# Attention scores in a one-core Fourier and latent-attention layer: three full-array passes replaced by two full ones and one on 32 rows, with queries and keys made earlier and parked in DRAM

## The chip, the cores and the metric

The kernel runs on one core of a Trainium2 chip. The metric is the device time of one execution in microseconds (us). The kernel before takes 936.31 us, the median of three runs (936.22 to 936.6).

## What is computed

One layer of a diffusion backbone on 1024 latent and 128 context tokens. Two branches leave one input projection: a Fourier mix over positions and channels, gated and mapped to 1024 channels (the output map), and latent attention with 8 heads. Both are merged with sigmoid gates, projected once more, added to the input and normalised. The part that the change touches is this:

```python
def mla_attention(q_nope, q_rope, k_nope, k_rope, v):
    ...
        s = jnp.einsum('bqhd,bkhd->bhqk', qn, k_nope) + jnp.einsum('bqhr,bkr->bhqk', qr, k_rope)
        p = jax.nn.softmax(s.astype(jnp.float32) * scale, axis=-1).astype(v.dtype)
        return jnp.einsum('bhqk,bkhd->bqhd', p, v)
...
def merge_out(x, gate, u_f, z_f, attn, z_a, g_f, g_a, w_f_out_l, w_a_out_l, w_out_l):
    y_f = (fourier_mix(u_f) * jax.nn.silu(z_f)) @ w_f_out_l
    y_a = (attn * jax.nn.silu(z_a)) @ w_a_out_l
    merged = jax.nn.sigmoid(g_f) * y_f + jax.nn.sigmoid(g_a) * y_a
    return x + gate * (merged @ w_out_l)
```

A head has 64 channels without position (nope) and 32 rotary channels (rope) in queries and keys. Latent queries see 128 cached context keys and 1024 latent keys; the 128 context queries see 128 context keys.

## The kernel before

Every matrix product is made to nearly float32 accuracy out of rounded halves: an operand x is split into hi (x rounded) and lo (x minus hi), and `mm3` (line 121) issues three TensorE passes, hi by hi, hi by lo and lo by hi, into one PSUM bank (lines 122, 125 and 126). A pass loads 128 columns of weights (LDWEIGHTS, PEld in the profile) and streams up to 512 columns past them. A Python program writes the instructions down; a list scheduler then sets each engine's order. It may bring later instructions ahead of one that waits, for a free PSUM bank say. There are eight PSUM banks (`MM`, line 101), and 43 SBUF buffers of 4.6 KB per partition (`U`, line 86) that tiles take in turn.

The stages in order of time: the input side, Fourier transform and gate projections (up to about 421 us); the **Fourier output map** (`for m in range(8)`, from line 1027); **attention** (8 heads); the **merge** (`merge_part`, line 1288); the last projection. SyncE (SP) issues nearly all DMAs, in one order.

The output map has 8 blocks m of 3 column thirds c, each 12 passes of 384 columns. Between the thirds stand other pieces: `low_tr` (line 947) transposes the latent rows of one token tile and makes the operands cqh, cql, kvh, kvl and the rotary key rows; `k_up` makes the nope keys of two heads (head pair 0 here), `q_chunk` the queries of a head for 384 tokens (head 0, first third, here), `value_map` the values. The residual gate's rows are made here too, by `ada_rows` (line 228): 8 products at four positions of 32 array columns, and `gate_row`.

Attention runs by head. A head has 9 steps of 128 queries; eight of them score three thirds of 384 keys (`Step.score`, line 1091), the ninth scores the context. Each third takes the three passes of `mm3`, with all 128 rows in use: 64 nope rows, 32 rotary rows times cosine and 32 swapped rotary rows times sine; the weights are the queries and the keys stream. VectorE (DVE) takes the minimum (line 1099), ScalarE (ACT) the exponential (line 1110), TensorE transposes the result (line 1131), ACT and DVE split it (lines 1132 and 109), TensorE multiplies with the values (lines 1151 and 1152). The strings `HSEQ` and `LSEQ` set the order in which a head's pieces are written. During a head h, `q_chunk` (Q in the string) makes the queries still missing and those of head h+1, `k_up` and `k_split` (K) the next keys, with splits on GpSimd (POOL).

Of the kernel before, what the change touches and what calls it, by code (L numbers as in the profile page):

```python
# [17 lines left out]
P = 128  # L18
# [41 lines left out]
VS = (3, 0, 0)  # L60


@with_exitstack
def kernel(ctx: ExitStack, tc: tile.TileContext, a: dict):
# [376 lines left out]
    def split_w(src, shape):  # L441
        raw = U(shape, F32, "wr")
        nc.sync.dma_start(raw, src)
        return split(raw)
# [7 lines left out]
    low_d = dram.tile([9, P, 448], F32, name="low_d")  # L452
# [54 lines left out]
    def low_out(c, pss):  # L507
# [8 lines left out]
        for j, ps in enumerate(pss):  # L516
            t = 3 * c + j
            row = H([P, 448], s="low")
            xk = ps[:, 384:416].rearrange("p (a b i) -> p a b i", a=2, b=2)
            if t < 8:  # L520
# [6 lines left out]
                for r in range(2):  # L527
                    dve.tensor_tensor(out=row[:, 384 + 32 * r : 416 + 32 * r], in0=t2.rearrange("p a b i -> p (a b i)"),
                                      in1=t1.rearrange("p a b i -> p (a b i)"), op=ALU.add)
            else:  # L530
                for r in range(2):
# [318 lines left out]
    def low_load(i):  # L850

        rows = U([P, 2, 448], s="low")
        for e in range(2):
# [3 lines left out]
            else:  # L857
                nc.sync.dma_start(row[:, 256:384], a["cache_ckv"])
                nc.sync.dma_start(row[:, 384:416], a["cache_krope"])
                nc.sync.dma_start(row[:, 416:448], a["cache_krope"])  # L860
# [26 lines left out]

    for i, (kind, dst, blk, m) in enumerate(PAIRS):
# [12 lines left out]

    gate_d = dram.tile([2, D], F32, name="gate_d")
    grow = [U([2, D], F32, "grow") for _ in range(2)]
    nc.sync.dma_start(grow[1], a["b_gate"].to_broadcast([2, D]))

    def load_gate(j):
        parts = []
        for q in range(4):
            w = U([P, 2, 512], s="wgate")
            nc.sync.dma_start(w, a["w_gate"][j, q])  # L910
            parts.append(w)
        return parts

    def gate_row(rows, j):
        ps = MM()
        pe.matmul(ps[0:2, :], sel, rows, start=True, stop=True)
        sl = slice(j * 512, (j + 1) * 512)
        dve.tensor_tensor(out=grow[0][:, sl], in0=ps[0:2, :], in1=grow[1][:, sl], op=ALU.add)
        if j == 1:
            nc.sync.dma_start(gate_d, grow[0])  # L920

# [4 lines left out]
    KB = [(U([P, NT], F32R, "kh"), U([P, NT], F32R, "kl")) for _ in range(2)]  # L926
    KC = [(C([P, P], F32R, "kch"), C([P, P], F32R, "kcl")) for _ in range(2)]
# [5 lines left out]
    def put_kv(ckvn, krd, kv_h, kv_l, kb, sl, gain=True):  # L933
# [3 lines left out]
        pe.transpose(pt[0:64, 128:256], krd, ident)  # L937
# [5 lines left out]
        for h, l in kb:  # L943
            act.copy(h[64:128, sl], pt[0:64, 128:256])
            dve.tensor_tensor(out=l[64:128, sl], in0=pt[0:64, 128:256], in1=h[64:128, sl].bitcast(F32), op=ALU.subtract)

    def low_tr(t, row):
        sl = slice(t * P, (t + 1) * P)
        ckn, kd = row[:, 256:384], row[:, 384:448]
        if t == 9:  # L950
            put_kv(ckn, kd, kvh[:, 1024:1152], kvl[:, 1024:1152], KB, slice(1024, 1152), False)
            return
        if t < 8:
            put_kv(ckn, kd, kvh[:, sl], kvl[:, sl], KB, sl)
        else:
            put_kv(ckn, kd, kch, kcl, KC, slice(0, 128))
# [14 lines left out]
    def k_up(wk, c, kf):  # L971
# [5 lines left out]
        mm3(ps[:, 0:n], wk[:, 0, :], wk[:, 1, :], rh, rl, True, True)  # L977
        for e in range(2):
            x = H([64, CH], s="kf") if e == 0 else None
            x = x[:, 0:n] if e == 0 else (kf[0][:, sl] if c < 3 else kf[1])  # L980
            act.copy(x, ps[64 * e : 64 * e + 64, 0:n])  # L981
            if e == 0:
                k_split(0, c, x)

    def k_split(e, c, x):
        if c < 3:
            sl = slice(c * CH, (c + 1) * CH)
            kh, kl = KB[e][0][0:64, sl], KB[e][1][0:64, sl]
        else:
            kh, kl = KC[e][0][0:64, :], KC[e][1][0:64, :]  # L990
# [518 lines left out]
```

## Time and profile before

| What | Value |
| --- | --- |
| median of three runs | 936.31 us |
| the profiled execution's own time | 938.17 us |
| its span in the profile | 936.4 us |
| TensorE busy / weight loads busy | 892.8 / 841.9 us |
| VectorE / ScalarE / GpSimd busy | 629.2 / 422.9 / 411.9 us |
| granted TensorE clock, mean over the span | 0.989 |
| DMA | 115.59 MB |

The median of the runs lies at the span of the profiled execution; that execution's own time is 1.8 us longer. "Busy" TensorE counts a pass from its issue to its modelled end, so passes overlap; the spacing of their starts is what a pass costs.

### The profile page before, as it was taken

Reading aid. Unit: us, or ns where it says so; the run is one execution under the profiler, and the core shown is the slowest. Engines: PE = TensorE matmul, PEld = TensorE weight load, DVE = VectorE, ACT = ScalarE, POOL = GpSimd, SP = SyncE. Lnnn points to the kernel's source line nnn. Section 1 sums busy time; section 2 is a strip of 40 time slices with the busy share of each in tenths; the row PEclk is TensorE's granted clock in tenths of the full one; section 3 lists DMA queues with packets and bytes.
Section 4 is the critical chain, followed back from the end, with each engine's and each line's share of the span. In section 5 each row is a group of like instructions: output and inputs, shape, how many; then the busy total and the mean of one; then the engine's idle time right before and its main releaser. Section 6 shows DMA issues by size and latency. Waiting matters only on the chain.

```text
span 936.4 us, 15839 instructions
## 1 busy us (share of the span) xinstructions
PE 892.8 (95%) x5814; PEld 841.9 (90%) x5814; DVE 629.2 (67%) x1276; ACT 422.9 (45%) x1149; POOL 411.9 (44%) x494
## 2 busy tenths in 40 slices
PE   4878999999999999999999999999999999999996
PEld 3667999899999999998899999999999989988885
DVE  3898466655545544658538889889889887784333
ACT  7555374411112211135128787787787782212111
POOL 1586313674444448942051263263263126763221
PEclk9889999999999999999999999999999999999999
DMA  9923645422222244278733000000000147342222
GB/s 365 361 89 120 229 144 188 155 97 96 97 97 96 97 146 146 97 280 295 268 139 135 7 7 4 7 7 4 7 7 2 62 182 280 107 157 90 91 92 88
DMA packets 35797, 115.59 MB, mean 123 GB/s; under 512 B 4484, under 2 KB 9348, under 8 KB 35720
## 3 DMA queue, kind: packets, MB, share of 16 engines
q1 hardware_dynamic: 31688, 105.94, 31.5%
q10 hardware_dynamic: 3168, 6.16, 1.8%
q0 software_dynamic: 864, 2.49, 0.8%
q8 instruction: 46, 0.75, 0.3%
q14 instruction: 31, 0.25, 0.1%
HBM read 81.74 MB, written 32.83 MB: 122 GB/s over the span
## 4 chain that ended last, share of the span: by engine, by line
PE 76%; POOL 4%; DVE 3%; DMA 1%; ACT 1%; issue 1%; DVEq 0%; SPq 0%; ACTq 0%; POOLq 0%
PE mm L122 21%; PE mm L126 20%; PE mm L125 20%; PE mm L1131 6%; PE mm L1152 4%; PE mm L1151 3%; POOL z L761 1%; POOL z L765 1%; DMA fz_d<-z 1%; DVE tl L109 1%; POOL wp L106 1%; DMA wr<-in_w_f_out 1%; POOL mfl L1295 1%; DVE hTl L109 0%; PE mm L1186 0%
## 5 line engine op out<-in xcount | busy, mean ns | idle before, releaser
L1099 DVE TENSOR_REDUCE s<-mm 128x1 f32<-128x384 f32 (+1 forms) x200 | 104.8, 540 | 15.6 <-PE mm L126 13.8
L109 DVE TENSOR_TENSOR tl<-mm,th 128x384 fp32r<-128x384 f32 (+1 forms) x216 | 102.9, 504 | 16.8 <-ACT th L1132 16.2
L1110 ACT ACTIVATE p<-mm,s 128x384 f32<-128x384 f32 x192 | 110.2, 588 | 7.3 <-DVE s L1104 7.1
L122 PE MATMUL mm<-hTh,wp 128*128 128x288 f32 x352 | 104.4, 297 | 0.0
L125 PE MATMUL mm<-hTl,wp 128*128 128x288 f32 x352 | 104.4, 297 | 0.0
L126 PE MATMUL mm<-hTh,wp 128*128 128x288 f32 x352 | 104.3, 297 | 0.0
L1132 ACT CAST th<-mm 128x384 fp32r<-128x384 f32 (+1 forms) x216 | 89.4, 461 | 25.6 <-PE mm L1131 22.7
L1131 PE MATMUL mm<-c,p 128*128 128x128 f32 x576 | 95.7, 274 | 1.9 <-ACT s L981 0.5
L1131 PEld LDWEIGHTS mm<-c,p 128*128 128x128 f32 x576 | 71.7, 140 | 9.0 <-DVE tl L109 1.8
L122 PE MATMUL mm<-th,wp 128*128 128x288 f32 x264 | 78.4, 297 | 1.3 <-ACT th L559 0.6
L125 PE MATMUL mm<-tl,wp 128*128 128x288 f32 x264 | 78.1, 296 | 1.5 <-DVE tl L109 1.5
L126 PE MATMUL mm<-th,wp 128*128 128x288 f32 x264 | 78.1, 296 | 0.0
L1152 PE MATMUL mm<-tl,v 128*128 128x384 f32 (+1 forms) x216 | 74.0, 346 | 0.2 <-DVE tl L109 0.2
L1151 PE MATMUL mm<-th,v 128*128 128x384 f32 (+1 forms) x216 | 73.2, 343 | 0.0
L122 PE MATMUL mm<-kh,q 128*128 128x384 f32 x192 | 70.7, 368 | 0.4 <-DVE tl L109 0.3
L122 PEld LDWEIGHTS mm<-hTh,wp 128*128 128x128 f32 x352 | 67.0, 190 | 0.3 <-ACT u L792 0.3
L125 PEld LDWEIGHTS mm<-hTl,wp 128*128 128x128 f32 x352 | 66.8, 190 | 0.0
L126 PEld LDWEIGHTS mm<-hTh,wp 128*128 128x128 f32 x352 | 66.8, 190 | 0.0
L125 PE MATMUL mm<-kl,q 128*128 128x384 f32 x192 | 64.7, 337 | 0.0
L126 PE MATMUL mm<-kh,q 128*128 128x384 f32 x192 | 64.0, 338 | 0.0
L106 POOL TENSOR_SCALAR q<-qf 128x384 fp32r<-128x384 f32 x24 | 12.3, 512 | 104.1 <-DVE qf L1004 65.4
L122 PE MATMUL mm<-hi,mh 128*128 128x512 f32 (+1 forms) x152 | 57.7, 383 | 0.0
(343 smaller groups left out, 2580.8 us busy)
## 6 DMA issues: line engine op xcount, KB each, us to landing
wr<-in_w_in SPq DMA_DIRECT2D x24, 512.0 KB, 4.2
x<-in_x_sample SPq DMA_DIRECT2D x16, 512.0 KB, 4.8
wada<-in_w_ada SPq DMA_DIRECT2D x16, 512.0 KB, 10.2
h_d<-hf SPq DMA_DIRECT2D x8, 576.0 KB, 3.3
gf_d<-z SPq DMA_DIRECT2D x8, 576.0 KB, 4.7
gfl<-gf_d SPq DMA_DIRECT2D x8, 576.0 KB, 4.6
mf_d<-mf SPq DMA_DIRECT2D x8, 576.0 KB, 3.2
gal<-ga_d SPq DMA_DIRECT2D x8, 576.0 KB, 3.7
```

Of the source, the lines that this page charges most:

```text
L106: pool.tensor_scalar(out=out, in0=x, scalar1=1.0, scalar2=1.0, op0=ALU.mult, op1=ALU.mult)
L109: dve.tensor_tensor(out=out, in0=x, in1=hi.bitcast(F32), op=ALU.subtract)
L122: i = pe.matmul(out, lh, rh, start=start, stop=False, skip_group_check=on)
L125: pe.matmul(out, lh, rl, start=False, stop=False, skip_group_check=on)
L126: pe.matmul(out, ll, rh, start=False, stop=stop, skip_group_check=on)
L761: pool.tensor_tensor(out=out, in0=out, in1=tmp, op=ALU.mult)
L1099: dve.tensor_reduce(out=self.nb if self.last else self.mx[:, kc : kc + 1], in_=ps[:, 0:n], axis=AX.X, op=ALU.min)
L1110: act.activation(self.p[:, kc * CH : kc * CH + n], self.ps[kc][:, 0:n], AF.Exp, scale=-1.0, bias=self.nb, accum_out=SSP[(self.h // 2) % 2] ...
L1131: pe.transpose(pt[:, j * P : (j + 1) * P], self.pr[j][:, kt * P : (kt + 1) * P], ident)
L1132: act.copy(th[:, i, 0:n], pt[:, 0:n])
L1151: pe.matmul(po[:, 0:n], V[kt][:, h, :], th[:, i, 0:n], start=(self.nv == 0), stop=False)
L1152: pe.matmul(po[:, 0:n], V[kt][:, h, :], tl[:, i, 0:n], start=False, stop=(self.nv == 8))
```

## The change

Scores. The key side keeps three tiles per head parity: KA holds the hi of 64 nope rows, the hi of 32 rotary rows and the lo of 32 rotary rows; KB the lo of 64 nope rows and, on the other 64 rows, their hi again; KR the hi of the 32 rotary rows four times over, in four groups of 32 rows. The query tile has three matching parts. Rotation is now applied to the query itself, so there are 96 rows per query, and hi by hi, hi by lo and lo by hi are 288 rows: two passes of 128 rows and one of 32. The 32-row passes of a step's three thirds stand at three positions of 32 array rows (`tile_position=(32 * g, 0)`) and are written one after another, ahead of the first third's full passes. A step takes its three PSUM banks at that point.

Queries and keys. All 24 query pieces (`q_up`) and all 16 key pieces (`k_up`) are made in the output map, by a table `TASKS` of 25 entries, one per column third and one behind. They are written to DRAM (`q_d`, `k_d`), and in attention `k_load` (6 DMAs a head) and `q_load` (7 DMAs a query tile) bring them in, at the places L and Q of the strings. The ten `low_tr` stand two to a third. The gate's rows move from the output map to the merge. The lo halves of the new weights are made on POOL.

```diff
+TASKS = (
+    "L0 L1", "L2 L3 W", "L4 L5 W", "L6 L7", "L8 L9 W", "k00 k01", "k02 k03 q00", "q01 q02 W", "k10 k11 k12", "k13 q10 q11 W", "q12 q20",
...
+)
...
-    KB = [(U([P, NT], F32R, "kh"), U([P, NT], F32R, "kl")) for _ in range(2)]
-    KC = [(C([P, P], F32R, "kch"), C([P, P], F32R, "kcl")) for _ in range(2)]
+    KB = [(U([P, NT], F32R, "ka"), U([P, NT], F32R, "kb")) for _ in range(2)]
+    KC = [(C([P, P], F32R, "kca"), C([P, P], F32R, "kcb")) for _ in range(2)]
+    KR = U([P, NT], F32R, "kr"), C([P, P], F32R, "kcr")
+    q_d = dram.tile([NH, 3, 96, 2, CH], F32, name="q_d")
+    k_d = dram.tile([4, P, 2, NT + P], F32, name="k_d")
...
-        for h, l in kb:
-            act.copy(h[64:128, sl], pt[0:64, 128:256])
-            dve.tensor_tensor(out=l[64:128, sl], in0=pt[0:64, 128:256], in1=h[64:128, sl].bitcast(F32), op=ALU.subtract)
+        act.copy(kr, pt[:, 128:256])
+        for k in kb:
+            act.copy(k[64:96, :], pt[64:96, 128:256])
+            lo_dve(k[96:128, :], pt[96:128, 128:256], kr[96:128, :])
...
+        mm3(ps[:, 0:n], wk[0][:, p, :], wk[1][:, p, :], rh, rl, True, True)
+        k = U([P, 2, CH], F32R, "k")
+        act.copy(k[:, 0, 0:n], ps[:, 0:n])
+        lo_dve(k[:, 1, 0:n], ps[:, 0:n], k[:, 0, 0:n])
+        nc.sync.dma_start(k_d[p][:, :, sl], k.bitcast(F32)[:, :, 0:n])
+
+    def k_load(h):
+        rows = slice(64 * (h % 2), 64 * (h % 2) + 64)
+        src = k_d[h // 2][rows]
+        for (ka, kb), sl in ((KB[h % 2], slice(0, NT)), (KC[h % 2], slice(NT, NT + P))):
+            nc.sync.dma_start(ka[0:64, :].bitcast(F32), src[:, 0, sl])
+            nc.sync.dma_start(kb[0:64, :].bitcast(F32), src[:, 1, sl])
+            nc.sync.dma_start(kb[64:128, :].bitcast(F32), src[:, 0, sl])
+
+    def q_up(h, c):
...
+        qf, qr = H([P, CH], s="qf"), H([P, CH], s="qr")
+        dve.tensor_tensor(out=qf[0:96, :], in0=ps[0:96, :CH], in1=TAB[0:96, sl], op=ALU.mult)
+        dve.tensor_tensor(out=qr[64:96, :], in0=ps[96:128, :CH], in1=TAB[96:128, sl], op=ALU.mult)
+        pool.tensor_tensor(out=qf[64:96, :], in0=qf[64:96, :], in1=qr[64:96, :], op=ALU.add)
+        q = U([96, 2, CH], F32R, "q")
+        act.copy(q[:, 0, :], qf[0:96, :])
+        lo_pool(q[:, 1, :], qf[0:96, :], q[:, 0, :])
+        nc.sync.dma_start(q_d[h, c], q.bitcast(F32))
+
+    def q_load(h, c):
+        t, src = U([P, 3, CH], F32R, "qt"), q_d[h, c]
+        for d0, d1, j, s0, i in ((0, 96, 0, 0, 0), (96, 128, 0, 64, 0), (0, 64, 1, 0, 0), (64, 128, 1, 0, 1),
+                                 (0, 32, 2, 64, 1), (32, 64, 2, 64, 1), (64, 96, 2, 64, 1)):
+            nc.sync.dma_start(t.bitcast(F32)[d0:d1, j, :], src[s0 : s0 + d1 - d0, i, :])
+        return t
...
+            if kc == 0:
+
+                n = P if self.last else CH
+                for g in range(1 if self.last else 3):
+                    ps = MM()
+                    rw = slice(32 * g, 32 * g + 32)
+                    pe.matmul(ps[:, 0:n], q[rw, 2, qs], KR[self.last][rw, n * g : n * g + n], start=True, stop=False, tile_position=(32 * g, 0))
+                    self.ps.append(ps)
             sl, n = (slice(0, P), P) if self.last else (slice(kc * CH, (kc + 1) * CH), CH)
-            kh, kl = (KC if self.last else KB)[e]
-            ps = MM()
-            mm3(ps[:, 0:n], q[:, 0, qs], q[:, 1, qs], kh[:, sl], kl[:, sl], True, True)
+            ps = self.ps[kc]
+            for i, k in enumerate((KC if self.last else KB)[e]):
+                pe.matmul(ps[:, 0:n], q[:, i, qs], k[:, sl], start=False, stop=(i == 1))
...
             elif o == "Q":
                 nq += 1
-                if nq < 3:
-                    qs[nq] = q_chunk(wq, nq)
+                if nq == 1:
+                    qs[2] = q_load(h, 2)
                 elif h + 1 < NH:
-                    q0 = q_chunk(wq1, 0)
+                    qn[nq - 2] = q_load(h + 1, nq - 2)
...
+    wgt, rows = [load_gate(0), load_gate(1)], []
     merge_open(0)
     merge_open(1)
...
         merge_open(m)
+        if m > 2 and rows:
+            gate_row(rows.pop(0), m - 3)
+        if wgt:
+            rows.append(ada_rows(wgt.pop(0), 2, 512, MM()))
```

The scheduler decides where the new passes stand. TensorE's order before, in head 0, at the third step's scores between value products (kh and kl are the keys' halves, q the queries, th, tl and v the probabilities' halves and the values; each mm number is one use of a PSUM bank):

```order
L1151 MATMUL mm_5439<-th_5442,v_5253 128x384
L122 MATMUL mm_5481<-kh_4524,q_5314 128x384
L125 MATMUL mm_5481<-kl_4525,q_5314 128x384
L126 MATMUL mm_5481<-kh_4524,q_5314 128x384
L1152 MATMUL mm_5439<-tl_5443,v_5253 128x384
L1151 MATMUL mm_5439<-th_5442,v_5272 128x384
L122 MATMUL mm_5486<-kh_4524,q_5314 128x384
L125 MATMUL mm_5486<-kl_4525,q_5314 128x384
L126 MATMUL mm_5486<-kh_4524,q_5314 128x384
L1152 MATMUL mm_5439<-tl_5443,v_5272 128x384
```

And the same place of TensorE in the changed kernel (line 1108 is the 32-row pass with kr, line 1113 a full pass with ka or kb, lines 1165 and 1166 the value products):

```order
L1165 MATMUL mm_5921<-th_5924,v_5742 128x384
L1108 MATMUL mm_5961<-kr_4548,qt_5658 128x384
L1113 MATMUL mm_5961<-ka_4540,qt_5658 128x384
L1113 MATMUL mm_5961<-kb_4541,qt_5658 128x384
L1166 MATMUL mm_5921<-tl_5925,v_5742 128x384
L1165 MATMUL mm_5921<-th_5924,v_5761 128x384
L1108 MATMUL mm_5963<-kr_4548,qt_5658 128x384
L1113 MATMUL mm_5963<-ka_4540,qt_5658 128x384
L1113 MATMUL mm_5963<-kb_4541,qt_5658 128x384
L1166 MATMUL mm_5921<-tl_5925,v_5761 128x384
```

The three 32-row passes of a step, written side by side, do not stand side by side: each stands alone ahead of its own bank's full passes. Over the whole program the 200 passes of line 1108 stand in 194 groups: 189 alone (181 of 384 columns, 8 of 128), four pairs and one group of three.

On SP's queue before, in the output map, from one load of w_f_out (wr, a block's weights) to the next (mf is a block's result, gfl the gate input, wgate the residual gate's weights):

```order
L839 DMA wr_4751<-in_w_f_out 128x512
L1060 DMA mf_d<-mf_4648 128x1152
L847 DMA gfl_4756<-gf_d 128x1152
L910 DMA wgate_4853<-in_w_gate 128x1024
L910 DMA wgate_4855<-in_w_gate 128x1024
L910 DMA wgate_4857<-in_w_gate 128x1024
L910 DMA wgate_4859<-in_w_gate 128x1024
L839 DMA wr_4861<-in_w_f_out 128x512
```

In the changed kernel, between two such loads on SP, there are stores of keys and queries (k_d, q_d), key loads for head 0 (ka, kca, kcb) that need those stores, and query weights (in_w_uq):

```order
L985 DMA k_d<-k_4887 256x1x128
L1009 DMA q_d<-q_4903 96x768
L991 DMA ka_4540<-k_d 64x1152
L991 DMA kca_4544<-k_d 64x128
L450 DMA wr_4953<-in_w_uq 128x2x256
L1067 DMA mf_d<-mf_4860 128x1152
L1009 DMA q_d<-q_4933 96x768
L992 DMA kcb_4545<-k_d 64x128
L1009 DMA q_d<-q_4949 96x768
L993 DMA kcb_4545<-k_d 64x128
L846 DMA wr_4998<-in_w_f_out 128x512
```

The load of w_f_out in the last row now waits its turn behind DMAs that themselves wait for stores and splits.

More of the change, by code (lines that the diff above doesn't have):

```diff
@@ L450, in load_r @@
         return t
[L452 removed]
+    low_d = dram.tile([9, P, 512], F32, name="low_d")
     f_d = dram.tile([4, P, NT], F32, name="f_d")
@@ L526, in low_out @@
                 dve.tensor_tensor(out=t2, in0=xk, in1=co, op=ALU.mult)
-                for r in range(2):
+                for r in range(4):
                     dve.tensor_tensor(out=row[:, 384 + 32 * r : 416 + 32 * r], in0=t2.rearrange("p a b i -> p (a b i)"),
@@ L530, in low_out @@
             else:
-                for r in range(2):
+                for r in range(4):
                     act.copy(row[:, 384 + 32 * r : 416 + 32 * r], ps[:, 384:416])
@@ L850, in low_load @@
     def low_load(i):
-        rows = U([P, 2, 448], s="low")
+        rows = U([P, 2, 512], s="low")
         for e in range(2):
@@ L858, in low_load @@
                 nc.sync.dma_start(row[:, 256:384], a["cache_ckv"])
-                nc.sync.dma_start(row[:, 384:416], a["cache_krope"])
-                nc.sync.dma_start(row[:, 416:448], a["cache_krope"])
+                for r in range(4):
+                    nc.sync.dma_start(row[:, 384 + 32 * r : 416 + 32 * r], a["cache_krope"])
         return rows
@@ L898 @@
         pair(b, nb_, kind, dst, m, fs, {} if nb_ else {0: fz_load, 1: low_loads, 7: gf_first, 5: fz_split})
[L902 to L914, printed above, removed]
-        ps = MM()
[L916 to L920, printed above, removed]
     cqh = [U([P, NT], F32R, "cqh") for _ in range(2)]
@@ L1026, with task @@
     nc.sync.dma_start(TAB, a["tab"])
+    wv, qs = [], {}
+    def task(k):
+        o, i = k[0], [int(x) for x in k[1:]]
+        if o == "L":
+            low_tr(i[0], lows[i[0] // 2][:, i[0] % 2])
+        elif o == "k":
+            k_up(*i)
+        elif o == "q":
+            q_up(*i)
+        elif o == "W":
+            up_weights()
+        elif o == "w":
+            wv.extend(split_w(a["w_uv"], [P, 512], lo_pool))
+        elif o == "K":
+            k_load(0)
+        elif o == "Q":
+            qs[i[0]] = q_load(0, i[0])
+        elif o == "v":
+            value_map(len(V))
     for m in range(8):
-        if m in (1, 3):
-            wgt = load_gate(m // 2)
-        elif m in (2, 4):
-            rows = ada_rows(wgt, 2, 512, MM())
         nxt = (load_half("w_f_out", m + 1), load_gf(m + 1)) if m < 7 else None
-        if m == 4:
-            wk, wq = load_split(a["w_uk"][0], P), load_split(a["w_uq"][0], 256)
-        if m == 5:
-            wvh, wvl = split_w(a["w_uv"], [P, 512])
-            kf = new_kf()
         mf = U([P, NT], F32, "mf")
@@ L1068 @@
         za.append(z)
-    for _ in range(3):
-        value_map(len(V))
+    for k in TASKS[24].split():
+        task(k)
     stage.close()
@@ L1297, in merge_part, with load_gate, gate_row @@
         lo_dve(ml[m][:, sl], mf[:, sl], mh[m][:, sl])
+    gate_d = dram.tile([2, D], F32, name="gate_d")
+    grow = [U([2, D], F32, "grow") for _ in range(2)]
+    nc.sync.dma_start(grow[1], a["b_gate"].to_broadcast([2, D]))
+    def load_gate(j):
+        parts = []
+        for q in range(4):
+            w = U([P, 2, 512], s="wgate")
+            nc.sync.dma_start(w, a["w_gate"][j, q])
+            parts.append(w)
+        return parts
+    def gate_row(rows, j):
+        ps = MM()
+        pe.matmul(ps[0:2, :], sel, rows, start=True, stop=True)
+        sl = slice(j * 512, (j + 1) * 512)
+        dve.tensor_tensor(out=grow[0][:, sl], in0=ps[0:2, :], in1=grow[1][:, sl], op=ALU.add)
+        if j == 1:
+            nc.sync.dma_start(gate_d, grow[0])
     def merge_open(m):
```

103 lines of the change are left out of this document (30 added, 73 removed), and 2 rows, old and new, of the table TASKS.

## The prediction

> **What bounds the kernel now.** First the page's busy times, then TensorE by stage (the windows), then the chain of work that ended last inside attention.
>
> ```profile
> PE 892.8 (95%) x5814; PEld 841.9 (90%) x5814; DVE 629.2 (67%) x1276; ACT 422.9 (45%) x1149; POOL 411.9 (44%) x494
> ```
>
> ```profile
> core 0: us, PE busy (x) PEld busy (x) DVE busy (x) ACT busy (x) POOL busy (x), PEclk, DMA share, GB/s
> 421.00:497.00 76.00, 75.58 (x438) 67.60 (x438) 47.82 (x104) 27.05 (x75) 21.87 (x31) 1.00 0.65 237
> 497.00:772.00 275.00, 272.73 (x1813) 262.39 (x1812) 237.79 (x575) 218.36 (x668) 102.52 (x172) 1.00 0.09 31
> 556.90:626.90 70.00, 69.69 (x466) 67.35 (x466) 60.38 (x146) 55.34 (x171) 29.38 (x50) 1.00 0.02 6
> 772.00:844.00 72.00, 69.84 (x384) 66.24 (x383) 56.80 (x75) 14.80 (x31) 48.53 (x44) 1.00 0.53 180
> ```
>
> ```profile
> 556.86 0.49 ACT th L1132
> 557.37 0.57 DVE tl L109
> 626.84 0.49 ACT th L1132
> 696.88 0.49 ACT th L1132
> ```
>
> The windows are, in order, the output map, attention, two heads of it, and the merge. TensorE is busy nearly throughout in all of them, at full granted clock (1.00), and VectorE is the next engine in attention with 60.4 of 70.0 us. In the chain the same ACT piece comes back at 556.86, 626.84 and 696.88: two heads take 70.0 us, and in that time the chain leaves TensorE for 0.49 and 0.57 us only. So attention and the output map cost what TensorE's passes cost, start to start. That spacing is read from the timeline, not from the 337 ns that a pass lasts, since passes overlap:
>
> ```profile
> 594.72 0.34 PE L122 MATMUL mm<-kh,q 128*128 128x384 f32 x1
> 594.89 0.34 PE L125 MATMUL mm<-kl,q 128*128 128x384 f32 x1
> 595.07 0.34 PE L126 MATMUL mm<-kh,q 128*128 128x384 f32 x1
> ```
>
> A full pass of 384 columns costs 0.174 us (0.35 for two), and its weight load is hidden beside the pass ahead.
>
> **The moved queries and keys: nothing on TensorE.** Query work leaves attention and enters the output map with the same passes. Of 24 query pieces 23 move: 23 x 6 passes x 0.174 = 24.0 us. Of the keys three head pairs of four move, each with 9 passes of 384 columns and 3 of 128 (0.11 each, the spacing of weight loads below): 3 x 1.90 = 5.7 us. Both stages are bound by TensorE, so 29.7 us go out of the one and into the other, sum 0.
>
> What hides the rest? Each query piece now takes two DVE products, where one took 0.55 us:
>
> ```profile
> L1004 DVE TENSOR_TENSOR qf<-mm,tab 128x384 f32<-128x384 f32 x24 | 13.2, 552 | 2.1 <-PE mm L126 1.2 <-PE mm L1131 0.4 <-issue 0.3
> L112 POOL TENSOR_TENSOR q<-qf,q 128x384 fp32r<-128x384 f32 x24 | 24.3, 1013 | 1.5
> ```
>
> The map grows to about 106 us (76.0 + 29.7). DVE there goes from 47.8 us to about 82 (47 more products and 16 key subtractions of at most 0.55 each), POOL from 21.9 to about 80 (24 pieces of two 1.0 us operations, and weight splits). TensorE still ends last on average, but with less cover. One place is thinner: the first five thirds now carry two `low_tr` each. In attention DVE, ACT and POOL only lose work.
>
> The DMAs of the round trip through DRAM fall in attention, where the DMA engines are used 9% of the time, and each query tile is asked for some steps ahead of its use. Bound: 0 to 2 us, taken as 0. The stores and key loads in the output map are another matter, because SP issues in order, and the map's weights already come late:
>
> ```profile
> L106 POOL TENSOR_SCALAR whl<-wr 128x512 fp32r<-128x512 f32 x16 | 9.9, 618 | 41.1 <-DMA wr<-in_w_f_out 38.0 <-DVE mf L1044 1.7 <-issue 1.4
> ```
>
> ```profile
> 436.82 5.44 DMA wr<-in_w_f_out
> ```
>
> Ahead of these splits POOL waited 41.1 us, 38.0 of them for the load (its group holds the merge's weights too), and once the chain runs through that load. In the changed order the load stands behind stores that wait for POOL's lo halves. What then waits is TensorE at the next block's first third. The gate weights (8 loads) leave that queue, which helps a little: below zero by at most the one wait, -5 us. I take +4 us, with -5 and +20 as bounds (half of the eight blocks waiting 5 us).
>
> The gate's products move to the merge with all their passes, 0 on TensorE; their sums and copies fall on DVE, with 56.8 of 72 us there. I take +1, bounds 0 and +4. Their 4 MB of loads go out during the last head.
>
> **The scores.** Nine passes a step become six full ones and three of 32 rows. Side by side at three positions, the three might run at once. But the order puts 189 of 200 alone, between full passes. So the count of passes is as before, and the question is the price of a lone narrow pass. The trace of before shows none of 32 rows. Nearest are passes of 63 rows in the Fourier stage, with the array rows left, the streamed columns right in "63*128 63x128". TensorE's timeline, then its weight loads:
>
> ```profile
> 125.27 0.27 PE L125 MATMUL mm<-cax,pq 66*128 66x128 f32 x1
> 125.38 0.27 PE L126 MATMUL mm<-cax,pq 66*128 66x128 f32 x1
> 125.58 0.33 PE L122 MATMUL mm<-cax,pq 63*128 63x128 f32 x1
> 125.75 0.27 PE L125 MATMUL mm<-cax,pq 63*128 63x128 f32 x1
> 125.86 0.27 PE L126 MATMUL mm<-cax,pq 63*128 63x128 f32 x1
> 126.06 0.46 PE L126 MATMUL mm<-hi,hTl 128*128 128x416 f32 x1
> 126.36 0.35 PE L122 MATMUL mm<-hi,hTh 128*128 128x416 f32 x1
> ```
>
> ```profile
> 125.32 0.19 PEld L126 LDWEIGHTS mm<-cax,pq 66*128 66x128 f32 x1
> 125.58 0.18 PEld L122 LDWEIGHTS mm<-cax,pq 63*128 63x128 f32 x1
> 125.69 0.19 PEld L125 LDWEIGHTS mm<-cax,pq 63*128 63x128 f32 x1
> 125.80 0.19 PEld L126 LDWEIGHTS mm<-cax,pq 63*128 63x128 f32 x1
> 126.06 0.19 PEld L126 LDWEIGHTS mm<-hi,hTl 128*128 128x128 f32 x1
> 126.17 0.19 PEld L122 LDWEIGHTS mm<-hi,hTh 128*128 128x128 f32 x1
> ```
>
> Within a kind the loads stand 0.11 us apart. At each border, 66 rows to 63 and 63 to 128, they stand 0.26 apart. So the first load of the new kind isn't brought ahead: it waits until the last pass of the old kind has streamed (0.11 load, 0.06 for 128 columns) and 0.09 more. The border needs rows of 64 or fewer: 96 to 66 rows shows no gap.
>
> ```profile
> 113.81 0.28 PE L654 MATMUL mm<-cax 96*97 96x256 f32 x1
> 113.93 0.23 PE L122 MATMUL mm<-cax,c 66*97 66x128 f32 x1
> ```
>
> A second place has it too, the gate's products on 32 array columns:
>
> ```profile
> 457.50 0.33 PE L126 MATMUL mm<-hi,whl 128*128 128x384 f32 x1
> 457.76 1.92 PE L231 MATMUL mm<-wgate,c 128*32 128x512 f32 x16
> 459.62 0.44 PE L122 MATMUL mm<-hi,whl 128*128 128x384 f32 x1
> 459.90 0.34 PE L125 MATMUL mm<-lo,whl 128*128 128x384 f32 x1
> ```
>
> The last full pass has streamed at 457.67, and the first narrow one starts 0.09 later; behind the block the next full pass has its follower 0.28 behind it, not 0.17: its load of 0.11 was uncovered.
>
> The Trainium skill, page "TensorEngine Tiling (Array Packing)", section "Key Properties", says that changing the tiling mode, not just the tile, drains TensorE. By that rule each lone pass pays on entering and on leaving. It gives no price; the 0.26 us gaps above agree with it. They do not at 63 weight columns, where the next full pass follows in 0.11 us:
>
> ```profile
> 71.15 0.28 PE L126 MATMUL mm<-wph,fol 128*63 128x252 f32 x1
> 71.26 0.28 PE L122 MATMUL mm<-wph,foh 128*128 128x260 f32 x1
> ```
>
> The price of a lone 32-row pass of 384 columns, from end of stream to the next start of stream: 0.09 drain, 0.11 load, 0.17 stream, 0.09 drain, 0.11 load, in all 0.57 us in place of 0.17. That is 0.40 more. For 128 columns: 0.46 in place of 0.11, 0.35 more. A pair, if it overlaps: 0.68 in place of 0.35, 0.33 more; the group of three 0.79 in place of 0.52. Sum: 181 x 0.40 + 8 x 0.35 + 4 x 0.33 + 0.27 = 76.8 us. Bounds of the price: 0 (32 rows behave as 66 do) and 0.45 (a drain of 0.115, if the first pass behind also starts late). I take 0.40, since 63 rows are the nearest kind, and both borders were measured.
>
> What goes in return: with TensorE at about 80 us for two heads (70.0 - 8.2 moved + 48 x 0.40), the two waits of 0.49 and 0.57 us vanish under the longer work of TensorE: -1.06 x 4 = -4 us.
>
> **Sum**: 76.8 - 4 + 4 + 1 = 78 us on a span of 936.4. The profiled execution's own time of 938.17 is 1.8 above its span, and the median of the runs, 936.31, is at the span. Forecast of the median: 936.3 + 78 = 1014 us.
>
> **Rivals.**
>
> *Half the price.* Only one border is paid, because a 32-row load can be brought ahead into array rows at another moment than a 63-row one. Then 0.20 for each of 194 groups is 39 us, and with the same +1 the time is 976. Against it: both borders in both places above cost. Chance 0.12.
>
> *No price.* Lone 32-row passes behave as those of 66 and 96 rows. Then the 77 us fall away, the moved 29.7 us still cancel, the waits of attention go by -4, since POOL, DVE and ACT are relieved there, and -5 if the gate loads' leaving frees w_f_out: 936.3 - 4 - 5 + 1 = 928, or 937 with the +4 of the map. It decides where the price of a group is below about 0.02 us (4 us over 194). Against it stand the 63-row gaps. Chance 0.06.
>
> *The three run side by side, as written.* Every triple would cost about one pass, 64 x 0.35 = 22 us less: 936.3 - 22 = 914. The gate's block speaks for such overlap on columns (16 passes of 512 columns in 1.92 us, 0.12 each). The order speaks against it: one triple in the program. The Trainium skill, page "TensorE: Matmul & The Clock Gate", Part 3, has four 32-row tiles at 512 columns run 3.07 times as fast as one after another; no run here shows it on rows, and by it the time would be near this rival's 914, if they were adjacent. Chance 0.02.
>
> *SP's queue becomes the bound in the output map.* If half of the blocks wait 5.4 us for w_f_out behind the stores, the +4 becomes about +20: 1030. For it: the row of 38.0 us of POOL waiting. Chance 0.10.
>
> *The clock falls.* With drains every half microsecond TensorE may be granted less:
>
> ```profile
> 23.40:46.80 23.40, 19.47 (x166) 15.13 (x166) 20.93 (x49) 13.02 (x24) 12.00 (x13) 0.85 0.93 361
> ```
>
> Early on, with idle stretches, it had 0.85. Attention would be 4 x 80 = 320 us; at 0.85 that is 56 more, 1070. The gaps here are far shorter than that stage's. Chance 0.03.
>
> **How the numbers follow.** Forecast 0.67, and the rivals as said. The range runs from the half price, 976, with the map gaining (-9 against the +4 taken), 967, to the SP rival with a price of 0.42, 1034; outside lie no price, side by side and the falling clock (0.11 together) and the tails of the forecast. A difference of 0.2% (1.9 us) is what a measurement of this kernel can tell from none. Faster by more: 0.06 (side by side, and most of no price). Within: 0.02. Slower: 0.92.
>
> **What would show it.** In the profile after: weight loads of line 1108 and of the first pass of line 1113 behind each standing about 0.26 us and more from their forerunner, two heads at about 79 us in the chain, the output map at about 106 us, DVE in attention below 75% busy, and w_f_out still in the chain. Two heads at 62 us would refute the price; attention as forecast with a map of 125 us would put the error on SP's queue; a granted clock below 0.95 in attention on the clock.

## The result, and the profile after

The changed kernel takes 1032.22 us (median, 1028.89 to 1034.57); the kernel before took 936.26 us (935.26 to 936.6) beside it. The ratio is 1.102, with an interval of 1.099 to 1.106. The forecast was 1014 us, so the direction is right and the size is 18 us short. The range went from 967 to 1034 us. The profiled execution took 1031.85 us and has a span of 1030.1 us.

Busy times of the whole span come first. TensorE is busy for 95% as before, with the same 5814 passes, but for 83 us longer.

```profile
PE 976.2 (95%) x5814; PEld 847.5 (82%) x5814; DVE 659.2 (64%) x1331; ACT 429.0 (42%) x1169; POOL 380.1 (37%) x417
```

The windows of the changed kernel follow, cut at the first pass of each stage: the output map, attention, two heads of it, the merge, and the rest of the span.

```profile
core 0: us, PE busy (x) PEld busy (x) DVE busy (x) ACT busy (x) POOL busy (x), PEclk, DMA share, GB/s
414.40:524.70 110.30, 103.34 (x573) 98.77 (x572) 76.51 (x162) 40.63 (x114) 70.20 (x72) 0.96 0.80 260
524.70:862.60 337.90, 328.22 (x1670) 240.62 (x1669) 242.31 (x564) 211.20 (x649) 27.47 (x59) 0.98 0.30 83
577.90:659.80 81.90, 80.29 (x420) 58.90 (x419) 60.05 (x140) 52.53 (x163) 7.11 (x15) 1.00 0.26 65
862.60:920.60 58.00, 56.57 (x327) 51.45 (x327) 42.44 (x57) 11.21 (x22) 37.63 (x35) 1.00 0.61 229
920.60:1030.10 109.50, 101.00 (x457) 82.01 (x456) 42.56 (x89) 19.00 (x53) 28.61 (x23) 0.98 0.31 106
```

Cut at the same passes, the kernel before has these windows. They start at the first pass itself, so they differ a little from the round ones of the prediction.

```profile
420.50:496.00 75.50, 75.08 (x436) 67.15 (x435) 47.33 (x103) 26.68 (x75) 22.25 (x31) 1.00 0.65 237
496.00:776.70 280.70, 277.10 (x1843) 266.35 (x1841) 243.32 (x589) 221.06 (x675) 104.02 (x175) 1.00 0.11 37
776.70:823.10 46.40, 45.57 (x258) 45.26 (x259) 34.89 (x45) 10.19 (x20) 35.08 (x33) 1.00 0.48 163
823.10:936.40 113.30, 105.74 (x488) 87.55 (x486) 51.24 (x96) 18.38 (x52) 32.19 (x24) 0.98 0.31 107
```

The two sets of rows give the account of the 93.7 us between the spans:

| Stage | before | after | difference | forecast |
| --- | --- | --- | --- | --- |
| up to the map's first pass | 420.5 | 414.4 | -6.1 | 0 |
| output map | 75.5 | 110.3 | +34.8 | +33.7 (29.7 + 4) |
| attention | 280.7 | 337.9 | +57.2 | +43.1 (-29.7 + 76.8 - 4) |
| merge and rest | 159.7 | 167.5 | +7.8 | +1 |
| sum | 936.4 | 1030.1 | +93.7 | +78 |

In the chain of waits of the changed kernel the same piece comes back every 81.8 us, where two heads took 70.0 before.

```profile
577.93 0.66 PE mm L1145 x6
...
659.78 0.65 PE mm L1145 x6
...
741.59 0.66 PE mm L1145 x6
```

TensorE's timeline in the changed kernel shows a lone narrow pass (line 1108) between full ones. The first number of a row is the start.

```profile
663.41 0.34 PE L1166 MATMUL mm<-tl,v 128*128 128x384 f32 x1
663.59 0.34 PE L1165 MATMUL mm<-th,v 128*128 128x384 f32 x1
663.86 0.44 PE L1108 MATMUL mm<-kr,qt 32*128 32x384 f32 x1
664.23 0.44 PE L1113 MATMUL mm<-ka,qt 128*128 128x384 f32 x1
664.50 0.34 PE L1113 MATMUL mm<-kb,qt 128*128 128x384 f32 x1
664.68 0.34 PE L1166 MATMUL mm<-tl,v 128*128 128x384 f32 x1
```

Full passes start 0.18 us apart. From 663.59 to 664.50 there are three steps, of 0.27, 0.37 and 0.27 us, together 0.91 where three full steps take 0.52. So 0.39 us are lost around this narrow pass. The weight loads of the same stretch show where:

```profile
663.41 0.19 PEld L1165 LDWEIGHTS mm<-th,v 128*128 128x128 f32 x1
663.86 0.18 PEld L1108 LDWEIGHTS mm<-kr,qt 32*128 32x128 f32 x1 [0.26 <-DVE tl L116]
664.22 0.19 PEld L1113 LDWEIGHTS mm<-ka,qt 128*128 128x128 f32 x1 [0.19 <-issue]
664.33 0.19 PEld L1113 LDWEIGHTS mm<-kb,qt 128*128 128x128 f32 x1
```

Between full passes a load is brought ahead (664.33 stands 0.11 behind 664.22, while its forerunner's pass streams). The narrow pass's load and that of the full pass behind it start only with their own passes. Summed over attention, the waits of the weight loads name the second kind 181 times (the columns are us in total, times, and the longest):

```profile
PEld mm L1113 <- issue: 34.1, 181, 0.3
PEld mm L1108 <- issue: 18.2, 79, 0.7
```

### The profile page after: what moved, and what is told of

Its sections match the earlier page's. It is cut to its first block, busy times and chain, and to the rows that moved or that the text cites. A ratio compares the mean times of both kernels' runs of the same rounds, so it can differ in the third digit from the quotient of the medians.

```text
span 1030.1 us, 16438 instructions
## 1 busy us (share of the span) xinstructions
PE 976.2 (95%) x5814; PEld 847.5 (82%) x5814; DVE 659.2 (64%) x1331; ACT 429.0 (42%) x1169; POOL 380.1 (37%) x417
## 4 chain that ended last, share of the span: by engine, by line
PE 68%; POOL 6%; DVE 4%; issue 3%; DMA 3%; ACT 3%; SPq 1%; DVEq 0%; POOLq 0%; ACTq 0%
PE mm L129 13%; PE mm L133 12%; PE mm L132 12%; PE mm L1113 10%; PE mm L1108 7%; PE mm L1145 6%; PE mm L1165 4%; PE mm L1166 3%; DMA wr<-in_w_f_out 1%; POOL z L768 1%; POOL mfl L1298 1%; POOL z L772 1%; DVE lo L116 1%; DMA fz_d<-z 1%; DMA q_d<-q 1%
## 5 line engine op out<-in xcount | busy, mean ns | idle before, releaser
L1114 DVE TENSOR_REDUCE s<-mm 128x1 f32<-128x384 f32 (+1 forms) x200 | 108.6, 545 | 70.5 <-PE mm L1113 68.2
L113 POOL TENSOR_SCALAR s<-s 128x128 f32<-128x128 f32 x36 | 10.2, 297 | 256.9 <-DVE s L1118 120.6
L1145 PE MATMUL mm<-c,p 128*128 128x128 f32 x576 | 91.0, 278 | 5.8 <-DVE osb L1179 1.9
L1113 PE MATMUL mm<-ka,qt 128*128 128x384 f32 x192 | 85.3, 444 | 0.0
L1108 PE MATMUL mm<-kr,qt 32*128 32x384 f32 x192 | 82.2, 444 | 0.3 <-DVE tl L116 0.2
L1108 PEld LDWEIGHTS mm<-kr,qt 32*128 32x128 f32 x192 | 34.1, 184 | 40.8 <-issue 17.1
L1113 PE MATMUL mm<-kb,qt 128*128 128x384 f32 x192 | 65.7, 342 | 0.0
```

Of the source, the lines that this page charges most:

```text
L1108: pe.matmul(ps[:, 0:n], q[rw, 2, qs], KR[self.last][rw, n * g : n * g + n], start=True, stop=False, tile_position=(32 * g, 0))
L1113: pe.matmul(ps[:, 0:n], q[:, i, qs], k[:, sl], start=False, stop=(i == 1))
L1114: dve.tensor_reduce(out=self.nb if self.last else self.mx[:, kc : kc + 1], in_=ps[:, 0:n], axis=AX.X, op=ALU.min)
L1145: pe.transpose(pt[:, j * P : (j + 1) * P], self.pr[j][:, kt * P : (kt + 1) * P], ident)
```

## The experiments

Four questions were open. Is the lost time the border between 32-row and full passes? Why did attention give back less than the 29.7 us that left it? What holds up the output map? What did the gates' move do? Each ratio compares a run with the kernel before, run beside it.

**The same narrow pass with 96 rows.** The two spare strips of rows are set to zero, so that the result stays as it is and the number of passes and columns too.

```
-  rw = slice(32 * g, 32 * g + 32)
-  pe.matmul(ps[:, 0:n], q[rw, 2, qs], KR[self.last][rw, n * g : n * g + n], ..., tile_position=(32 * g, 0))
+  pe.matmul(ps[:, 0:n], q[0:96, 2, qs], KR[self.last][0:96, n * g : n * g + n], start=True, stop=False)
```

> The changed kernel with each narrow pass streamed over 96 array rows instead of 32 (the two other copies of the keys set to zero, same result), so with no narrow row mode at all, and the same 200 passes, round trip through DRAM and output map. Border theory (a lone 32-row pass pays 0.40 us at its two borders): 194 groups x 0.40 = 77 us go, 1032 becomes about 955, and if the clock losses of attention were a consequence, down to 948. Rival (three PSUM banks held at once and the DMA trips slow attention): attention stays as it is, 1025 to 1035.

It took 966.63 us, ratio 1.033 (1.031 to 1.035). The border costs 65.6 us of the changed kernel's time; over 194 groups that is 0.34 us each. But 31 us over the kernel before stay, which the border theory alone does not give. Its attention, in the windows:

```profile
525.10:794.90 269.80, 257.21 (x1670) 240.49 (x1668) 231.81 (x563) 210.30 (x649) 27.46 (x59) 0.99 0.38 105
```

**The three narrow passes side by side.** The full passes come first, the three narrow passes of a step stand together behind them, and the reductions follow.

```
+  for g, ps in enumerate(self.ps):
+      rw = slice(32 * g, 32 * g + 32)
+      i = pe.matmul(ps[:, 0:n], q[rw, 2, qs], KR[self.last][rw, n * g : n * g + n], start=False, stop=True, tile_position=(32 * g, 0))
+      tc.keep_in_program_order(i)
```

> The changed kernel with the narrow passes behind a step's full passes, pinned so that all 64 triples stand side by side. Border theory with overlap at three positions: 0.27 us more than three full passes for each triple, 64 x 0.27 + 8 x 0.35 = 20 us instead of 77, so about 975. Border theory without overlap (three streams of 0.17 one after another): 0.39 for each, 28 us, about 983, and the narrow passes start 0.17 us apart. The theory that the narrow mode is slow in itself (each pass pays, wherever it stands): 1030.

It took 978.75 us, ratio 1.046 (1.044 to 1.047). TensorE's timeline of this kernel shows one group of three:

```profile
526.27 0.34 PE L1106 MATMUL mm<-kb,qt 128*128 128x384 f32 x1
526.54 0.44 PE L1111 MATMUL mm<-kr,qt 32*128 32x384 f32 x3
526.91 0.44 PE L1106 MATMUL mm<-ka,qt 128*128 128x384 f32 x1
527.19 0.34 PE L1106 MATMUL mm<-kb,qt 128*128 128x384 f32 x1
```

From 526.27 to 527.19 are 0.92 us, of which the two full passes take 0.35. So the three narrow passes cost 0.57 us together, with both borders. A lone one costs 0.56 (0.91 - 0.35) in the changed kernel, so the three do run at once. But three full ones take 0.52, so the borders eat more than the overlap gives: 64 groups lose 64 x 0.05 = 3 us. The expectation had 0.27 us of loss for a group and a 96-row form of 955 us; its 975 lies near the measured time because these two errors cancel. This kernel is 12 us slower than the one with 96 rows. Its attention is 284 us long with TensorE busy for 265 of them, so it waits for 19 us where the 96-row form waits for 13; that the reductions come only behind the third narrow pass is a likely reason, not a shown one.

**The border in the kernel before, at 64 and at 96 rows.** In the kernel before, one of the three passes of each third of a score is cut to 64 rows in the one run and to 96 in the other, and stands first. The product of the rows that are cut off is left out; nothing else changes.

```
-  mm3(ps[:, 0:n], q[:, 0, qs], q[:, 1, qs], kh[:, sl], kl[:, sl], True, True)
+  pe.matmul(ps[:, 0:n], q[0:64, 0, qs], kl[0:64, sl], start=True, stop=False)
+  pe.matmul(ps[:, 0:n], q[:, 0, qs], kh[:, sl], start=False, stop=False)
+  pe.matmul(ps[:, 0:n], q[:, 1, qs], kh[:, sl], start=False, stop=True)
```

> The kernel before, with one of the three score passes (hi query by lo key) cut to the first 64 array rows, so part of the scores' correction is left out; it is written first and 199 of these passes stand alone or nearly. Nothing else of the change is in it. Border theory: 192 x 0.40 + 8 x 0.35 = 80 us on 936, about 1012 (1005 to 1016). Rival (the cost lies in the moved queries and keys and the DRAM trips): 936.

> The control for the 64-row cut: the same kernel with that pass cut to 96 array rows (part of the correction left out). Border theory: 96 rows are no mode of their own, 936. If any pass with fewer than 128 rows pays: about 1012 here too.

With 64 rows it took 1009.69 us, ratio 1.079 (1.077 to 1.081); with 96 rows 936.29 us, ratio 1.0011 (1.0001 to 1.0021). In a stage where TensorE has no slack, 200 lone passes of 64 rows cost 74 us, 0.37 each, and 200 of 96 rows nothing. So the price belongs to the border, not to the maps, the loads or the position argument of the changed kernel.

**One bank at a time.** In the changed kernel the narrow passes of a step take three PSUM banks ahead of the first full pass. Here each third takes its bank when its own passes come, with 96 rows and with 32.

```
-  for g in range(1 if self.last else 3):
-      ps = MM()
-      ...
+  ps = MM()
+  pe.matmul(ps[:, 0:n], q[0:96, 2, qs], KR[self.last][0:96, sl], start=True, stop=False)
```

> The kernel with 96-row narrow passes (966.6), but each third of a score takes its PSUM bank only when its own three passes come, as before, instead of all three banks at the first narrow pass. It does what the kernel before does in the attention, less the query and key maps. Theory A (the 20 us by which its attention of 270 us is longer than the 247 to 251 left of 280.7 after the maps are taken out come from holding three banks early): about 947. Theory B (the maps were the work that covered the waits for ScalarE and VectorE, and their going costs it): unchanged, 964 to 969. Between these the share of each can be read off.

> The changed kernel with its 32-row passes, each third's narrow pass standing directly ahead of its own two full ones with a bank taken then. The price of the lone pass is the same, 65.6 us over the 96-row form. Theory A (early banks cost): the 96-row form of this run plus 66, about 1013. Theory B (the maps' cover): 1030 to 1034, as the changed kernel.

With 96 rows it took 961.39 us, ratio 1.027 (1.024 to 1.029), with 32 rows 1027.85 us, ratio 1.096 (1.091 to 1.101). That is 5 and 4 us less than with three banks at once (for 32 rows the intervals overlap), where theory A asked for 20. So early banks are at most a small part of the cause. The price of the border comes out a second time: 66.5 us over 200 lone passes, 0.33 each. The windows of the 96-row form, map and attention:

```profile
415.80:523.20 107.40, 100.42 (x575) 95.98 (x574) 75.85 (x162) 40.63 (x115) 72.69 (x76) 1.00 0.81 265
523.20:788.90 265.70, 254.88 (x1669) 236.26 (x1668) 229.81 (x565) 209.78 (x650) 27.43 (x59) 1.00 0.38 107
```

Attention is 265.7 us at full clock, with neither border nor held banks. Without the moved maps it should have 280.7 - 29.7 = 251.0.

**The maps left out.** In the kernel before, heads 1 to 7 use the queries of head 0 and the keys are not made anew. The weight loads and splits for them go too; the lines here show the queries.

```
-  if nq < 3:
+  if h == 0 and nq < 3:
       qs[nq] = q_chunk(wq, nq)
-  elif h + 1 < NH:
-      q0 = q_chunk(wq1, 0)
```

> The kernel before with 21 of the 23 query pieces and the 3 key pairs of the attention left out (heads 1 to 7 use the queries of head 0, and the keys are not made anew), nothing put in their place; by the prices of the prediction 21.9 + 5.7 = 27.6 us of TensorE passes. Theory A (the maps were cover: passes that TensorE ran while scores waited for ScalarE and VectorE, so that their going leaves waits of 10 to 15 us, as in the version with 96 rows and a bank for each third): 919 to 924. Theory B (taking them out costs nothing, and what is lost in the changed kernel's attention comes from its loads or its placing): 907 to 911.

It took 919.62 us, ratio 0.981 (0.979 to 0.983): 17 us less for 27.6 us of passes, as theory A had it. Its attention, in the windows:

```profile
496.30:760.10 263.80, 254.90 (x1685) 238.44 (x1683) 230.58 (x566) 210.72 (x651) 30.56 (x63) 1.00 0.10 34
```

Nothing was put anywhere else in this kernel, and no loads were added, yet attention stops at 263.8 us. The line of sums of the chain of waits shows who has come in. Attention of the kernel before, then of this one:

```profile
by line: PE mm L1131 21.5%; PE mm L122 16.2%; PE mm L126 15.7%; PE mm L125 15.5%; PE mm L1152 11.8%; PE mm L1151 11.5%; DVE tl L109 1.5%; PE mm L1186 1.4%; ACT th L1132 0.9%; DVE s L1099 0.9%; ACT p L1110 0.6%; issue 0.5%; DVE osb L1165 0.4
```

```profile
by line: PE mm L1131 16.1%; PE mm L1151 11.6%; PE mm L122 10.5%; PE mm L126 10.1%; PE mm L125 10.0%; ACT p L1110 9.7%; PE mm L1152 9.7%; DVE tl L109 5.3%; ACT th L1132 5.2%; DVE s L1099 3.9%; issue 2.1%; ACT ob L1164 1.3%; DVE osb L1165 1.2
```

The exponential (ACT p) goes from 0.6 to 9.7% of the chain, its transposed copies (ACT th, DVE tl) and the minimum (DVE s) rise with it. That fits theory A: the maps were passes that TensorE could run while a step's softmax was under way.

**The narrow pass left out.** This asks what the stacking could give at best.

```
-  pe.matmul(ps[:, 0:n], q[0:96, 2, qs], KR[self.last][0:96, sl], start=True, stop=False)
-  pe.matmul(ps[:, 0:n], q[:, i, qs], k[:, sl], start=False, stop=(i == 1))
+  pe.matmul(ps[:, 0:n], q[:, i, qs], k[:, sl], start=(i == 0), stop=(i == 1))
```

> The changed kernel without its narrow passes (the product of the rotary queries' lower halves with the rotary keys is left out) and with a bank for each third: what the stacking could give if the narrow pass were free. 200 passes fewer than the version with 96 rows and a bank for each third (961.4): 192 of 384 columns at 0.174 us and 8 of 128, about 34 us. Theory A (TensorE bounds the attention there too): about 927. Theory B (with the maps gone, ScalarE and VectorE bound it, so that less than half of the saved passes shows): 943 to 952.

It took 959.3 us, ratio 1.025 (1.024 to 1.027). 34 us of passes went, and 2 us of time: less even than theory B said. Its attention window, and the line of sums of its chain:

```profile
523.70:789.10 265.40, 235.30 (x1470) 206.36 (x1468) 228.59 (x566) 210.18 (x651) 27.73 (x60) 0.97 0.38 109
```

```profile
by line: ACT p L1117 16.6%; PE mm L1106 12.0%; PE mm L1138 11.4%; DVE s L1107 10.9%; DVE tl L116 9.2%; PE mm L1158 7.9%; ACT th L1139 6.9%; PE mm L1159 6.8%; issue 3.3%; DMA qt<-q_d 2.4%; DVE osb L1172 2.2%; DMA kb<-k_d 1.9%; ACT ob L1171 1
```

Attention is 265.4 us again, though TensorE is busy for only 235 of them, and the exponential leads the chain. Three kernels with 1685, 1669 and 1470 passes in attention have 264 to 266 us there: a floor of this list of steps, about 65 us for two heads. In the third kernel the clock of 0.97 can explain at most about 8 us (0.03 x 265.4, an estimate), so at full clock it would take 257 us or more. No engine is full in it (VectorE is busy for 229 of 265 us, ScalarE for 210), which points to the chain of one step into the next, and not to one engine's throughput. No run shortened that chain, so this reading is not tested. In the kernels that park queries and keys the chain also passes through their loads (2.4 and 1.9% in the line above).

**w_f_out on another queue.** The eight loads are issued by ScalarE, so that they don't stand behind the stores on SyncE.

```
-  nc.sync.dma_start(raw, a[name][m])
+  (nc.scalar if name == "w_f_out" else nc.sync).dma_start(raw, a[name][m])
```

> The changed kernel with the eight w_f_out loads issued on ScalarE's queue instead of SyncE's, so that they no longer stand behind the stores of q and k. Theory A (the order of SyncE's queue holds the loads back and makes most of the 8 us of TensorE waits and of the 4 us of lower clock in the output map): map from 110 to about 100 us, time about 1022. Theory B (the waits come from VectorE and GpSimd, which are slower to give the split weights, the queries and the keys): map 108 to 112, time 1029 to 1034. Slower than 1034 would say that the wait moved to ScalarE's own order.

It took 1028.93 us, ratio 1.100 (1.095 to 1.105). Map and attention in its windows:

```profile
414.50:524.70 110.20, 101.94 (x574) 97.12 (x572) 78.29 (x163) 40.48 (x114) 70.00 (x72) 0.98 0.79 260
524.70:857.00 332.30, 322.05 (x1670) 234.80 (x1669) 241.09 (x562) 211.18 (x649) 27.42 (x59) 1.00 0.30 85
```

The map is as long as before this edit, 110.2 against 110.3 us, as in theory B: the order of SyncE's queue does not set its length. It does not clear the loads themselves. In the changed kernel 12.6% of the chain inside the map runs through w_f_out's loads, and with this edit it is still 12.8%. So whether these loads set the length, or what theory B names, stays open. The second row is worth more: TensorE's passes in attention stand in the same order as in the changed kernel, and attention is 5.6 us shorter, at a granted clock of 1.00 instead of 0.98.

**The gates back in the map.** The gates' loads, products and rows stand again where the kernel before has them.

```
+  if m in (1, 3):
+      wgt = load_gate(m // 2)
+  elif m in (2, 4):
+      rows = ada_rows(wgt, 2, 512, MM())
```

> The changed kernel with the adaptive gates' loads, products and rows back in the output map, where the kernel before has them. Theory A (the gates in the merge cost more than their 6.4 us of passes, since VectorE and GpSimd bound the merge there): merge from 58 back to about 46.5 us, map from 110 to at most 117, time 1024 to 1029. Theory B (the gates' passes fill TensorE waits in the map): map stays near 110, time about 1020 to 1022. Theory C (they only move): 1030 to 1034.

It took 1040.44 us, ratio 1.112 (1.106 to 1.118), slower than all three theories said. Map, merge and rest in its windows:

```profile
415.00:541.80 126.80, 113.58 (x610) 101.89 (x608) 79.73 (x164) 42.09 (x116) 69.47 (x72) 0.95 0.77 261
...
877.50:923.80 46.30, 45.48 (x260) 45.16 (x259) 35.43 (x47) 10.65 (x21) 36.04 (x34) 1.00 0.51 178
923.80:1037.50 113.70, 105.70 (x488) 87.52 (x486) 51.23 (x96) 18.39 (x52) 32.18 (x24) 0.98 0.31 107
```

Merge and rest are 160.0 us, within 0.3 of the kernel before: so the whole +7.8 us there is the gates. But the map grows by 16.5 us. About 6 of them are the gates' own passes. TensorE also waits there for a gate's input, and for weights of the map that come later:

```profile
PE mm L936 <- ACT ada L247: 4.1, 1, 4.1
PE mm L129 <- POOL whl L113: 2.9, 2, 2.5
```

**Another order of the map's tasks.** Two lists for the 96-row form with a bank for each third (961.4 us): one row block in each third instead of two, queries mixed with keys, and values earlier. In the second list the weights are also asked for earlier.

```
-  "L0 L1", "L2 L3 W", "L4 L5 W", "L6 L7", "L8 L9 W", "k00 k01", "k02 k03 q00", ...
+  "L0 W", "L1 W", "L2", "L3 q00", "L4 k00 q10 W", "L5 q20 k10", "L6 q30 W", "L7 q01 k20", ...
+  "W L0 W", "L1 W", "L2", "L3 k00", "L4 q00 W", "L5 q10 k10", "L6 q20", "L7 q30 k20", ...
```

> The version with 96 rows and a bank for each third (961.4), with the list of tasks beside the output map spread: one low row block for each third instead of two, queries and keys mixed so that each third holds 1 to 2 us of them, values earlier and with queries between them. Theory A (the map's 8 to 9 us over its passes are waits of a few crowded places: two row blocks at once, values at the end): map from 107.4 to about 100 us, time about 954. Theory B (VectorE, GpSimd and the loads hold TensorE up wherever the tasks stand): map 105 to 110, time 959 to 964.

> The version with 96 rows and a bank for each third (961.4) with the spread list of tasks again, but the weights of w_uk and w_uq asked for two to four thirds ahead of their first use; in the first spread list TensorE waited 10.9 us for their upper halves. Theory A (the map's 8 to 9 us over its passes come from the order of the tasks, and a list without crowded places and late weights loses most of them): map from 107.4 to 99 to 103 us, time 953 to 957. Theory B (VectorE, GpSimd and the loads hold TensorE up in any order): map 105 to 110, time 959 to 964.

The first list took 969.71 us, ratio 1.034 (1.031 to 1.036): its own new wait was for the late weights of w_uq, whose upper half GpSimd splits.

```profile
PE mm L129 <- POOL hi L113: 10.9, 3, 5.4
```

The second took 953.78 us, ratio 1.020 (1.019 to 1.022). That is the time of theory A, but not by its way. Map and attention of this kernel:

```profile
414.40:521.40 107.00, 100.84 (x574) 96.92 (x574) 78.53 (x164) 41.13 (x114) 73.82 (x76) 0.98 0.82 268
521.40:784.60 263.20, 253.61 (x1670) 236.29 (x1668) 228.60 (x562) 209.99 (x649) 27.52 (x59) 1.00 0.38 108
```

The map is 107.0 us, against 107.4 with the list as written. The span is 5.9 us shorter in small pieces: 1.4 ahead of the map, 0.4 in it, 2.5 in attention, 1.6 behind. So the order of tasks did not shorten the map, and why the rest is shorter stays open. This is the fastest kernel that keeps the idea of the change and the whole computation, and it is still 2% slower than the kernel before. No version tried that computes everything beats that one.

## Why the prediction was right, and where it fell short

*The size.* The measured 1032 us lie only 2 us inside the range. Its upper end was drawn for loads that wait in SyncE's queue, together with a price of 0.42 us, and the runs show neither; that the range holds the time is luck. The mechanism that makes most of the 96 us, the price of a lone pass, is no luck. The 18 us that are missing are mainly waits (11 us off the forecast) and a lower clock (6) in attention and the gates in the merge (7), less the 6 us gained ahead of the map.

*Attention and map bound by TensorE, so that the moved passes sum to 0.* This step failed at both ends. TensorE ended last in the attention before, but only just: with the 29.7 us of passes gone and no borders, only 15 us come off (265.7 us), and two heads go from 70.0 to about 65 us. In the map the same passes cost more than their sum (below). The prediction saw the two waits of 0.49 and 0.57 us and took them to vanish under slower TensorE work (-4).

*The price of the lone pass.* The mechanism was right: both borders cost, the weight loads there stand 0.45 and 0.36 us from their forerunners, and 96 rows have no border. The unit in the timeline is 0.39 us where 0.40 was said; two heads take 81.8 us where 79 was said, and VectorE is busy for 72% of attention, below the 75% named. By this unit 189 lone passes are 74 us of TensorE, close to the 76.8 of the sum; in the kernel before, with less slack, 200 passes cost 74 us, 0.37 each. Against the 96-row form the changed kernel loses less, 65.6 or 66.5 us. That the longer passes cover a part of the waits of the 96-row form is the likely reason; no run separates it. The rivals of half the price and of no price are refuted by this. The rival of three side by side left the borders out: kept together they take 0.57 us, not 0.17. The Trainium skill, page "TensorEngine Tiling (Array Packing)", section "Key Properties", says that a change of the tiling mode drains TensorE, without a price. The runs agree with it for 64 rows (0.37 us) as for 32 (0.39 us in the timeline).

*The round trip through DRAM.* Taken as 0 with a bound of 2 us, and borne out: attention without it is 263.8 us (maps left out) and with it 265.7 or 263.2 us (96 rows, two lists of tasks). It is not free everywhere: in the 265.7 us the chain passes once through a load of keys for 5.2 us.

*The waits in attention.* Forecast -4. At full clock the changed kernel's attention is 332.3 us (the run with w_f_out on another queue). The passes give 280.7 - 29.7 + 74 = 325.0, so the waits grew by about 7 us. The clock adds 5.6. Together -29.7 + 74 + 7.3 + 5.6 = +57.2, the measured difference; the 7.3 is what the other terms leave. Without the borders these waits are larger: attention with 96 rows is 269.8 us, 18.8 over the 251.0 of passes.

*The clock.* The rival was put at 1070 us, with the clock low all through attention. What came is a small part of it: at some places TensorE runs at half clock for several us, here behind two waits. The windows and the timeline of the changed kernel at one such place:

```profile
810.00:815.00 5.00, 3.48 (x16) 2.05 (x15) 2.29 (x6) 3.94 (x13) 0.00 (x0) 0.83 0.01 3
815.00:820.00 5.00, 5.00 (x15) 3.46 (x15) 2.73 (x7) 1.80 (x7) 0.00 (x0) 0.50 0.00 0
```

```profile
811.43 0.77 PE L1145 MATMUL mm<-c,p 128*128 128x128 f32 x4 [0.93 <-DVE osb L1179]
812.79 1.32 PE L1145 MATMUL mm<-c,p 128*128 128x128 f32 x6 [0.59 <-DVE tl L116]
...
815.59 0.68 PE L1108 MATMUL mm<-kr,qt 32*128 32x384 f32 x1
816.20 0.69 PE L1113 MATMUL mm<-ka,qt 128*128 128x384 f32 x1
```

At a clock of 0.50 the narrow pass's follower stands 0.61 us behind it instead of 0.37. The borders do not bring this on: two heads with 48 lone passes ran at 1.00. Nor does one such wait: in the run with w_f_out on another queue the wait of 0.93 us stands at the same place, and all of attention has 1.00. What decides it is not shown.

*The output map.* Its length was put at about 106 us and is 110.3, but two errors nearly cancel in that. The text counted 76.0 + 29.7 and forgot that the gates' passes leave the map; with the 7.5 us that they take in the merge (a wait of 1.4 among them), the passes give 75.5 - 7.5 + 29.7 = 97.7. Over that lie about 10 us at full clock (107.4 in the 96-row form) and 3 us of lower clock. The +4 for SyncE's queue is not borne out: with the loads on another queue the map is as long, so the rival of SyncE's queue as the bound falls too. The waits that TensorE has there are single ones, mostly for VectorE:

```profile
PE mm L129 <- DVE qr L1004: 2.0, 1, 2.0
PE mm L129 <- DVE v L116: 1.9, 1, 1.9
PE mm L129 <- DVE ka L116: 1.3, 1, 1.3
```

Two other orders of the tasks moved these waits without shortening the map, so what holds it at 107 us is not settled.

*The gates.* Forecast +1 in the merge, measured +7.8, since the passes themselves were forgotten on that side as well. Their way out of the crowded map was worth more than that: with them back in it the time is 8 us longer.

*Ahead of the map* the changed kernel is 6.1 us earlier. Kernels with the front part of the kernel before reach the map at 418.2 to 420.9, those with the changed one at 413.5 to 416.0, so 2 us of this at least are steady. It was not tested what gives them.

## What to carry to other kernels

Before work is taken out of a stage, ask what the stage would cost without it. A stage where the busiest engine is at 99% can still have another chain a few per cent below, and a run with that work simply left out shows it for the price of one kernel. Before small passes are packed into strips of rows, count the borders. Here a 32- or 64-row pass alone among full passes cost about three full ones (0.17 + 0.39 us against 0.17), and padding it with zeros to 96 rows was cheaper. Three strips side by side ran at once and still cost slightly more than three full passes; longer groups were not tried.

## What the runs showed of the hardware

A pass of 64 rows between full ones costs 0.37 us more than one of 96 rows of the same columns, which costs as much as a full one (ratio 1.0011 over 200 of them). Three 32-row passes at different positions, one behind the other, run at once and take 0.57 us with both borders, as long as one alone, against 0.52 for three full passes. Behind two waits of TensorE, of 0.93 and 0.59 us, the granted clock was 0.83 and then 0.50 in two stretches of 5 us. Over the same order of passes in attention it was 0.98 in one execution and 1.00 in another.
